# Seven products instead of eight in six more blocks of a hybrid encoder layer's matrix products, and two more first weight blocks on ScalarE's queue

## The chip, the cores and the metric

The kernel runs on one core of one Trainium2 chip. Its time is the device time of one execution in microseconds (us). A core has five engines that work side by side, each through its own queue, in order: TensorE (PE, with PEld for the weight load that runs ahead of a matmul), VectorE (DVE), ScalarE (ACT), GpSimd (POOL) and SyncE (SP, which here only issues transfers). Matmuls add into banks of PSUM; everything else is in SBUF tiles. A matmul of a 128x128 stationary tile with 128x512 moving columns is the unit of the matrix work below.

## The reference, cut to what matters

One layer over 256 positions of 2048 channels, all in float32:

```python
u = rmsnorm(h, norm_mix[l])
z = u @ w_in[l]                       # 2048 x 11264: pool, q, k, v, ret. gate, two branch gates
y_pool = pool_branch(p, w_pool_group[l], pool_scale[l]) @ w_pool_proj[l]
y_ret = retention_branch(q, k, v, g_ret, ret_gn_gain[l]) @ w_ret_proj[l]
merged = jax.nn.sigmoid(g_pool_br) * y_pool + jax.nn.sigmoid(g_ret_br) * y_ret
h = h + merged @ w_out[l]
h = h + conv_glu(rmsnorm(h, norm_ffn[l]), w_up[l], conv_w[l], conv_b[l], w_down[l])
out = rmsnorm(h, norm_final)
```

The retention branch normalizes each head's result (a group norm), multiplies it by a silu gate and goes through `w_ret_proj`. The feed-forward part has 5632 channels, `w_up` twice that. Nearly all arithmetic is in the products with `w_in`, `w_ret_proj`, `w_out`, `w_up` and `w_down`, and all their weights (285.8 MB read in all) are used once.

## The kernel before, in words

**Three matmuls for one product.** To keep float32 accuracy, each operand is split into a high part (`hi`, rounded) and the rest (`lo`). `mm3` makes a product from three matmuls: high by high (L104), high weights by low activations (L105), low weights by high activations (L106). Weights come from memory as raw blocks of 128x2048 (1 MB, pool `wraw`, three buffers) and are split on the way: ACT copies 1024 columns into a `hi` tile (L96), DVE subtracts for the `lo` tile (L97). The pools `hi` and `lo` have four buffers of 1024 columns each. A buffer comes free with the last matmul that reads it, and the next block's split waits for that.

**Groups.** One raw block is a *group*: 256 rows of the inner dimension by 1024 output columns, 2x2 quarters of weights against 2x2 quarters of activations (two halves of the positions, `tb`). A *pair* (`run_pair`, `down_pair`) is 1024 output columns with all its groups: eight for `w_in` (eleven pairs), `w_ret_proj` (two) and `w_out` (two), 22 for `w_down` (two pairs). A plain group is eight products, 24 matmuls. A group that is listed as a *Strassen group* takes seven products, 21 matmuls (`Pair.seven`, `Pair.strassen`): sums of weight quarters are made on DVE (L304 128x1024, L306 and L311 128x512) and split like the rest, with a tile `four` (128x512 high and low together) that takes a buffer of the `hi` pool, and a tile for the sums `t13` from the pool `units`. The products come in the order p1, p2, p6, p3, p7, p5, p4; p1 and p2 read the first `hi` tile, p6 and p3 the second, p7 and p5 the split `t13`, p4 the tile `four`. Four of them (p1, p5, p6, p7) add up over all Strassen groups of a pair in four PSUM banks of their own; after the last such group `fix_steps` or `h_steps` (L437, L351) add them to the results.

**Sums of activations.** The products p6, p3, p7 and p5 need sums of activation quarters. `sums_of` prepares them once for each group number of `w_in` (used by all its pairs), of `w_ret_proj` and of `w_out`: L360 forms hi+lo, `sums` (L344 to L347) adds on DVE, then ACT and DVE split. For `w_down` they are made while `w_up` runs.

**What sets the order.** Work beside the matrix products (the retention itself, rotations, norms, transposes, the sums) is in closures in a list, `side`; `run_pair` takes one after each group (`tick`), and `flush` the rest. The engines' instruction streams are fixed ahead of time by a scheduler that lists the work by readiness and by priority: weight loads and splits come 128 places early (`weights_first`), result steps 64 (`results_first`). So the order within an engine's queue differs from the order of the source, and at run time each engine takes its queue strictly in order.

**The pairs of `w_in`, counted from 0:** 0 and 3 are q and k (first and second half of the heads), 1 and 4 are v, 2 and 5 the retention gate, 6 the pool input, 7 and 8 the pool branch's gate, 9 and 10 the retention branch's gate. Pair 0 runs as the input arrives: `load_x` and `load_w` (L159 to L165) issue the first transfers in a fixed order, the ones that follow on SP.

**The end.** The two pairs of `w_down` follow `w_up`, whose 44 steps (L878 with 128x512, L886 with 128x256) make the activations in 22 groups; `plain_a` and `sums_a` say where each group's are stored.

Of the kernel before, what the change touches and what calls it, by code (L numbers as in the profile page):

```python
# [9 lines left out]
F32R = mybir.dt.float32r  # L10
# [6 lines left out]
P = 128  # L17
D = 2048
T = 256
# [14 lines left out]
STRASSEN = (2, 4, 6, 8, 11, 13, 16, 18)  # L34
STRASSEN_Z = (1, 3, 5)
STRASSEN_R = (1, 3, 5)
# [12 lines left out]
def tile_block(ctx: ExitStack, tc: tile.TileContext, ins, out):  # L49
# [119 lines left out]
    tc.keep_in_program_order(load_w(0, 2, 1))  # L169
    tc.keep_in_program_order(load_x(1, 1))  # L170
    tc.keep_in_program_order(load_w(0, 0, 1))
    tc.keep_in_program_order(load_w(0, 3, 1))
# [180 lines left out]
    def sums_of(pair_hl, groups):  # L353

        dst = [unit(F32R), unit(F32R)]

        def of(i, g):
            f = t2k()
            o = slice(g % 4 * NB, (g % 4 + 1) * NB)
            dve.tensor_tensor(f, *(plain(x[g // 4][:, o]) for x in pair_hl), ALU.add)  # L360
            a11, a21, a12, a22 = (f[:, j * P : (j + 1) * P] for j in range(4))
            sums(a11, a12, a21, a22, [x[:, i * NB : (i + 1) * NB] for x in dst])

        s4 = {
            g: [[z[:, i * NB + j * P : i * NB + (j + 1) * P] for z in dst] for j in range(4)]
            for i, g in enumerate(groups)
        }
        return s4, [lambda i=i, g=g: of(i, g) for i, g in enumerate(groups)]
# [228 lines left out]
    def group_norm(half, o_all, mv, sg):  # L597
# [35 lines left out]
        side.append(lambda: (scale(), apply(0)))  # L633
        side.append(lambda: apply(1))
        side.append(lambda: apply(2))
        side.append(lambda: (turn((0, 1)), apply(3)))
# [9 lines left out]
    for half in range(2):  # L646
        qk = [unit(F32R), unit(F32R)]
        qk_pair(qk, STRASSEN_Z[2:] if half else (), None if half else first)
        vh, vl = unit(F32R), unit(F32R)
        if half == 0:  # L650
            zs, fill = sums_of((uh, ul), STRASSEN_Z)
            side.extend(fill)
        split_pair(vh, vl, STRASSEN_Z[1:2] if half else ())
# [3 lines left out]
        gate_pair(sg, AF.Silu, STRASSEN_Z[1:], apart=True)  # L657
# [5 lines left out]
    split_pair(ph, pl, STRASSEN_Z[1:2])  # L663
# [66 lines left out]
    for dst in (sgp, sgp, sgr, sgr):  # L730
        dst.append(unit())
        gate_pair(dst[-1], AF.Sigmoid, STRASSEN_Z if len(sgp) > 1 else STRASSEN_Z[2:])
# [20 lines left out]
    side.extend(fill)  # L753
    for p in range(2):
# [21 lines left out]
        if p == 0:  # L776
            os, fill = sums_of((mg_h, mg_l), STRASSEN_O)
            side.extend(fill)
# [72 lines left out]

    ah = [unit(F32R) for _ in range(7)]
    al = [unit(F32R) for _ in range(7)]
    plain_groups = [g for g in range(NFF // 2) if g not in STRASSEN]
# [7 lines left out]
    def sums_a(g, c):  # L862

        n = STRASSEN.index(g)
        o = n % 2 * 7 * P
# [3 lines left out]
    for j in range(NFF):  # L869
# [51 lines left out]
        else:  # L921
            dve.tensor_tensor(cs[:, 2 * P :], c, u, ALU.mult)
            a21, a11, a12, a22 = (cs[:, i * P : (i + 1) * P] for i in range(4))
            split(*sums_a(grp, slice(0, 3 * P)), cs[:, P:])
# [241 lines left out]
```

## Time and profile before

| | |
|---|---|
| three timed runs, median (lowest to highest) | 1454.62 us (1453.79 to 1455.55) |
| the profiled execution's own time | 1455.32 us |
| its span in the trace | 1453.5 us, so 1.8 us lie outside it |
| PE busy | 1442.0 us, 99% |
| DVE busy | 1178.4 us, 81% |
| ACT busy | 794.3 us, 55% |
| mean granted TensorE clock | 0.998 |
| read from memory | 285.82 MB, 200 GB/s over the span |

The busy rows give the sum of an engine's instruction times, their share of the span and the number of instructions. A row of the groups gives line, engine, operation, out<-in, shapes, a count, then the busy time of the group, the mean of one in ns, and the idle time just before them with what ended most of it. A row of a timeline gives the start in us, the duration in us, engine, line, operation, out<-in, shapes and a count; in brackets at its end stands the idle time before it and what ended that. A matmul's duration is longer than the distance to the next, since they overlap.

### The profile page before, as it was taken

How to read it: one execution, taken by the hardware profiler on the slowest of the kernel's cores; microseconds unless marked ns; L12 is line 12 of the kernel's file. 1: busy time of each engine (PE TensorE's matmuls, PEld its weight loads, DVE VectorE, ACT ScalarE, POOL GpSimd, SP SyncE). 2: the span in 40 equal slices, each digit the busy share in tenths (PEclk: the TensorE clock that was granted, in tenths of full speed). 3: DMA queues.
4: the chain of work that ended last, by engine and by line, in shares of the span. 5: the costliest groups of instructions: out<-in, count | busy, mean ns of one | idle time of the engine just before them, and what ended most of it. 6: DMA issues, size and time to landing. Idle time of an engine off the chain costs nothing.

```text
span 1453.5 us, 18725 instructions
## 1 busy us (share of the span) xinstructions
PE 1442.0 (99%) x7163; PEld 1221.0 (84%) x7163; DVE 1178.4 (81%) x1638; ACT 794.3 (55%) x1023; POOL 0.2 (0%) x4
## 2 busy tenths in 40 slices
PE   9999999999999999999999999999999999999997
PEld 6888888888888888888888888888888888888886
DVE  6778797987988888988877787777777778888877
ACT  6555654565665555555555555554555555555553
POOL 0000000000000000000000000000000000000000
PEclk9999999999999999999999999999999999999999
DMA  9664455554555656555555445545554556665663
GB/s 352 214 218 174 154 197 193 192 205 179 181 201 196 229 177 217 213 204 203 213 210 204 184 176 200 204 175 179 207 194 174 187 205 239 209 216 186 220 217 117
DMA packets 43289, 291.22 MB, mean 200 GB/s; under 512 B 4928, under 2 KB 5568, under 8 KB 9152
## 3 DMA queue, kind: packets, MB, share of 16 engines
q1 hardware_dynamic: 42480, 288.73, 55.3%
q10 hardware_dynamic: 720, 1.31, 0.3%
q8 instruction: 56, 0.92, 0.2%
q14 instruction: 33, 0.27, 0.0%
HBM read 285.82 MB, written 4.19 MB: 200 GB/s over the span
## 4 chain that ended last, share of the span: by engine, by line
PE 97%; DVE 1%; DMA 1%; ACT 0%; SPq 0%; issue 0%; DVEq 0%; ACTq 0%
PE acc L878 22%; PE acc L106 15%; PE acc L104 15%; PE acc L105 15%; PE acc L886 12%; PE aux L104 6%; PE aux L106 6%; PE aux L105 6%; DMA raw<-in_w_in 1%; DVE lo L97 1%; PE aux L804 0%; PE aux L526 0%; PE aux L744 0%; PE aux L623 0%; DVE u L351 0%; PE aux L687 0%
## 5 line engine op out<-in xcount | busy, mean ns | idle before, releaser
L96 ACT ACTIVATE hi<-raw 128x1024 fp32r<-128x1024 f32 (+1 forms) x522 | 545.8, 1052 | 404.5 <-PE acc L105 183.0
L97 DVE TENSOR_TENSOR lo<-raw,hi 128x1024 fp32r<-128x1024 f32 (+1 forms) x522 | 618.1, 1214 | 155.8 <-ACT hi L96 98.4
L104 PE MATMUL acc<-hi,u 128*128 128x512 f32 x926 | 362.1, 391 | 1.5 <-ACT hi L96 1.5
L106 PE MATMUL acc<-lo,u 128*128 128x512 f32 x926 | 360.8, 390 | 0.0
L105 PE MATMUL acc<-hi,u 128*128 128x512 f32 x926 | 360.5, 389 | 0.0
L878 PE MATMUL acc<-u,hi 128*128 128x512 f32 x1408 | 328.4, 390 | 0.0
L878 PEld LDWEIGHTS acc<-u,hi 128*128 128x128 f32 x1408 | 261.3, 188 | 52.2
L104 PEld LDWEIGHTS acc<-hi,u 128*128 128x128 f32 x926 | 173.9, 188 | 37.6 <-ACT hi L96 2.4
L106 PEld LDWEIGHTS acc<-lo,u 128*128 128x128 f32 x926 | 173.8, 188 | 37.5 <-DVE lo L97 1.3
L105 PEld LDWEIGHTS acc<-hi,u 128*128 128x128 f32 x926 | 173.9, 188 | 35.2
L886 PEld LDWEIGHTS acc<-u,lo 128*128 128x128 f32 x1408 | 174.8, 192 | 3.4
L886 PE MATMUL acc<-u,lo 128*128 128x256 f32 x1408 | 176.0, 283 | 0.0
L104 PE MATMUL aux<-hi,u 128*128 128x512 f32 x270 | 105.3, 390 | 0.0
L105 PE MATMUL aux<-hi,u 128*128 128x512 f32 x270 | 105.1, 389 | 0.0
L106 PE MATMUL aux<-lo,u 128*128 128x512 f32 x270 | 105.1, 389 | 0.0
L900 ACT ACTIVATE t<-acc 128x256 f32<-128x256 f32 x88 | 33.9, 385 | 100.1 <-PE acc L886 100.1
L96 ACT ACTIVATE u<-u 128x1024 fp32r<-128x1024 f32 x45 | 47.5, 1057 | 26.7 <-DVE u L304 22.3
L106 PEld LDWEIGHTS aux<-lo,u 128*128 128x128 f32 x270 | 50.7, 188 | 10.6
L104 PEld LDWEIGHTS aux<-hi,u 128*128 128x128 f32 x270 | 50.7, 188 | 10.5 <-ACT hi L96 0.2
L105 PEld LDWEIGHTS aux<-hi,u 128*128 128x128 f32 x270 | 50.7, 188 | 10.4
L96 ACT ACTIVATE four<-raw 128x512 fp32r<-128x512 f32 x43 | 27.2, 632 | 55.4 <-PE acc L105 20.8
L97 DVE TENSOR_TENSOR u<-u,u 128x1024 fp32r<-128x1024 f32 x45 | 54.9, 1221 | 3.1 <-ACT u L96 3.1
(181 smaller groups left out, 1098.2 us busy)
## 6 DMA issues: line engine op xcount, KB each, us to landing
raw<-in_w_up SPq DMA_DIRECT2D x88, 1024.0 KB, 5.0
raw<-in_w_in SPq DMA_DIRECT2D x85, 1024.0 KB, 4.9
raw<-in_w_down SPq DMA_DIRECT2D x44, 1024.0 KB, 4.9
raw<-in_w_ret_proj SPq DMA_DIRECT2D x16, 1024.0 KB, 4.9
raw<-in_w_out SPq DMA_DIRECT2D x16, 1024.0 KB, 4.9
raw<-in_w_pool_proj SPq DMA_DIRECT2D x8, 1024.0 KB, 4.9
u<-in_x SPq DMA_DIRECT2D x4, 1024.0 KB, 7.6
raw<-in_w_in SPq DMA_DIRECT2D x4, 512.0 KB, 8.4
```

The lines of the kernel that those rows point to most:

```text
L96: act.activation(hi, src, AF.Copy)
L97: dve.tensor_tensor(lo, src, plain(hi), ALU.subtract)
L104: pe.matmul(o, ah, bh, start=start, stop=False)
L105: pe.matmul(o, al, bh, start=False, stop=False)
L106: pe.matmul(o, ah, bl, start=False, stop=stop)
L878: pe.matmul(o[half], w2[half][hf][0][:, i * P : (i + 1) * P], hview(kt), start=kt == 0, stop=False)
L886: pe.matmul(o[half][:, :T], wl, hview(kt)[:, :T], start=False, stop=kt == KT - 1)
L900: act.activation(small_part[:, half * T : (half + 1) * T], o[half][:, T:], AF.Copy)
```

## The change

It enlarges the lists of Strassen groups: in the second q and k pair (group 5 becomes 4 and 5), in the second retention gate (3 and 5 become 3, 4 and 5), in both `w_ret_proj` pairs (1, 3, 5 become 1, 2, 4, 5) and in both `w_down` pairs (eight groups become nine, now every second group from 2 to 18). That is six groups more. The sums of activations of group 1 of `w_in`, which only the pairs 8 to 10 read, leave the list that runs during pair 1 (the sums for group 4 take their place there) and are made at the end of pair 7 or later. The ninth sums of `w_down` are stored in tiles that are free by then (`front`, `trig`, `trig_r` and what the last `ah`/`al` tiles have left), which takes one split more. The side work of the group norm is regrouped into fewer steps. At the start two 128x512 quarters of the first weight block are issued by ACT's queue instead of SP's.

```diff
-STRASSEN = (2, 4, 6, 8, 11, 13, 16, 18)
-STRASSEN_Z = (1, 3, 5)
-STRASSEN_R = (1, 3, 5)
+STRASSEN = (2, 4, 6, 8, 10, 12, 14, 16, 18)
+STRASSEN_Z = (1, 3, 4, 5)
+STRASSEN_R = (1, 2, 4, 5)
 STRASSEN_O = (2, 3)
...
     tc.keep_in_program_order(load_w(0, 1, 1, act))
-    tc.keep_in_program_order(load_w(0, 2, 1))
+    tc.keep_in_program_order(load_w(0, 2, 1, act))
     tc.keep_in_program_order(load_x(1, 1))
     tc.keep_in_program_order(load_w(0, 0, 1))
-    tc.keep_in_program_order(load_w(0, 3, 1))
+    tc.keep_in_program_order(load_w(0, 3, 1, act))
...
-        return s4, [lambda i=i, g=g: of(i, g) for i, g in enumerate(groups)]
+        return s4, {g: lambda i=i, g=g: of(i, g) for i, g in enumerate(groups)}
...
-        side.append(lambda: (scale(), apply(0)))
-        side.append(lambda: apply(1))
-        side.append(lambda: apply(2))
-        side.append(lambda: (turn((0, 1)), apply(3)))
+        side.append(lambda: (scale(), apply(0), apply(1)))
+        side.append(lambda: (apply(2), apply(3)))
+        side.append(lambda: turn((0, 1)))
         side.append(lambda: None)
         side.append(lambda: turn((2, 3)))
...
-        qk_pair(qk, STRASSEN_Z[2:] if half else (), None if half else first)
+        qk_pair(qk, (4, 5) if half else (), None if half else first)
         vh, vl = unit(F32R), unit(F32R)
         if half == 0:
             zs, fill = sums_of((uh, ul), STRASSEN_Z)
-            side.extend(fill)
-        split_pair(vh, vl, STRASSEN_Z[1:2] if half else ())
+            side.extend(fill.pop(g) for g in (3, 5, 4))
+        split_pair(vh, vl, (3,) if half else ())
...
-        gate_pair(sg, AF.Silu, STRASSEN_Z[1:], apart=True)
+        gate_pair(sg, AF.Silu, (3, 4, 5) if half else (3, 5), apart=True)
...
-        gate_pair(dst[-1], AF.Sigmoid, STRASSEN_Z if len(sgp) > 1 else STRASSEN_Z[2:])
+        if len(sgp) == 1:
+            side.append(fill.pop(1))
+        gate_pair(dst[-1], AF.Sigmoid, (1, 3, 5) if len(sgp) > 1 else (5,))
         flush()
...
     ah = [unit(F32R) for _ in range(7)]
     al = [unit(F32R) for _ in range(7)]
+    a1 = [const.tile([P, n], F32R, tag=tag, name=f"a1_{tag}") for tag, n in (("front", KT + T), ("trig", T))]
+    last22 = const.tile([P, T], F32R, tag="trig_r", name="last22")
...
         n = STRASSEN.index(g)
+        if n == 8:
+            if c.start >= 3 * P:
+                o = (22 % 8) * T - 3 * P
+                return [x[6][:, o + c.start : o + c.stop] for x in (ah, al)]
+            if c.start == 2 * P:
+                return [last22[:, :P], last22[:, P:]]
+            return [x[:, c] for x in a1]
...
-            split(*sums_a(grp, slice(0, 3 * P)), cs[:, P:])
+            for c in (slice(0, 2 * P), slice(2 * P, 3 * P)) if grp == STRASSEN[-1] else (slice(0, 3 * P),):
+                split(*sums_a(grp, c), cs[:, P + c.start : P + c.stop])
```

**Where the order moves: pair 8, the second pool gate, on DVE.** Of the change, from the low part of group 3's first half: raw_646 is group 3's raw block, lo_649 and lo_651 its two low tiles, four_653 its `four`; t_617 and t_618 are the sums of activations of group 1; raw_654 is group 4, lo_656 its first low tile, raw_659 is group 5.

```order
L97 TENSOR_TENSOR lo_649_3461<-raw_646_3456,hi_648_3460 128x1024
L101 SCALAR_TENSOR_TENSOR u_539_2890<-aux_616_3296,vecs_237,u_538_2889 128x256
L311 TENSOR_TENSOR raw_646_3456<-raw_646_3456 128x512
L97 TENSOR_TENSOR lo_651_3466<-raw_646_3456,hi_650_3465 128x1024
L360 TENSOR_TENSOR t_617_3325<-u_5_104,u_7_106 128x512
L344 TENSOR_TENSOR t_618_3327<-t_617_3325 128x128
L97 TENSOR_TENSOR four_653_3473<-raw_646_3456,four_653_3473 128x512
L345 TENSOR_TENSOR t_618_3327<-t_618_3327,t_617_3325 128x128
L304 TENSOR_TENSOR u_660_3533<-raw_659_3531 128x1024
L346 TENSOR_TENSOR t_618_3327<-t_617_3325 128x128
L97 TENSOR_TENSOR lo_656_3500<-raw_654_3497,hi_655_3499 128x1024
```

Of before, the same place (raw_638 is group 3's block there, raw_646 group 4's, raw_651 group 5's):

```order
L97 TENSOR_TENSOR lo_641_3438<-raw_638_3433,hi_640_3437 128x1024
L101 SCALAR_TENSOR_TENSOR u_533_2876<-aux_610_3282,vecs_237,u_532_2875 128x256
L97 TENSOR_TENSOR lo_643_3443<-raw_638_3433,hi_642_3442 128x1024
L311 TENSOR_TENSOR raw_638_3433<-raw_638_3433 128x512
L97 TENSOR_TENSOR four_645_3450<-raw_638_3433,four_645_3450 128x512
L304 TENSOR_TENSOR u_652_3510<-raw_651_3508 128x1024
L306 TENSOR_TENSOR raw_651_3508<-raw_651_3508,u_652_3510 128x512
L97 TENSOR_TENSOR lo_648_3477<-raw_646_3474,hi_647_3476 128x1024
```

The sums of group 1 (L360, L344 and on) now stand behind group 3's low tiles; before, they stood in pair 1.

**On PE in the same pair,** the change reads: two products of group 3 (p1 and p2 with hi_648), its p4 (four_653), and the first halves of group 4 (hi_655) and, further on, its second (hi_657), ahead of group 1's p6, which reads group 1's second tile hi_637 and the sums u_70:

```order
L104 MATMUL acc_620_3339<-hi_648_3460,u_5_104 128x512
L105 MATMUL acc_620_3339<-hi_648_3460,u_7_106 128x512
L106 MATMUL acc_620_3339<-lo_649_3461,u_5_104 128x512
L104 MATMUL acc_622_3341<-four_653_3473,u_5_104 128x512
L105 MATMUL acc_622_3341<-four_653_3473,u_7_106 128x512
L106 MATMUL acc_622_3341<-four_653_3473,u_5_104 128x512
L104 MATMUL acc_620_3339<-hi_655_3499,u_6_105 128x512
...
L104 MATMUL acc_623_3342<-hi_657_3503,u_6_105 128x512
L105 MATMUL acc_623_3342<-hi_657_3503,u_8_107 128x512
L104 MATMUL aux_631_3379<-hi_637_3390,u_70_473 128x512
L104 MATMUL acc_621_3340<-hi_637_3390,u_70_473 128x512
```

Of before, p2 of group 1 (hi_627), then its p6 and p3 (hi_629 is its second tile) and, a few rows on, its `four`:

```order
L104 MATMUL acc_612_3316<-hi_627_3362,u_5_104 128x512
L105 MATMUL acc_612_3316<-hi_627_3362,u_7_106 128x512
L106 MATMUL acc_612_3316<-lo_628_3363,u_5_104 128x512
L104 MATMUL aux_623_3356<-hi_629_3367,u_70_473 128x512
L105 MATMUL aux_623_3356<-hi_629_3367,u_71_474 128x512
...
L104 MATMUL acc_614_3318<-four_632_3375,u_5_104 128x512
```

The products of group 1 that need sums have moved from their own group to the middle of group 4; hi_637 is read by nothing earlier.

**Pair 5, the second retention gate, on DVE.** Of the change, from group 3's `four` (four_426): raw_427 is group 4's block, a Strassen group now, raw_435 group 5's.

```order
L97 TENSOR_TENSOR four_426_2254<-raw_419_2237,four_426_2254 128x512
L97 TENSOR_TENSOR lo_430_2283<-raw_427_2278,hi_429_2282 128x1024
L97 TENSOR_TENSOR lo_432_2288<-raw_427_2278,hi_431_2287 128x1024
L311 TENSOR_TENSOR raw_427_2278<-raw_427_2278 128x512
L304 TENSOR_TENSOR u_436_2321<-raw_435_2319 128x1024
L97 TENSOR_TENSOR four_434_2295<-raw_427_2278,four_434_2295 128x512
L97 TENSOR_TENSOR lo_438_2324<-raw_435_2319,hi_437_2323 128x1024
L306 TENSOR_TENSOR raw_435_2319<-raw_435_2319,u_436_2321 128x512
L97 TENSOR_TENSOR u_441_2332<-u_436_2321,u_441_2332 128x1024
```

Of before (raw_424 is the plain group 4, raw_429 group 5):

```order
L97 TENSOR_TENSOR four_423_2247<-raw_416_2230,four_423_2247 128x512
L97 TENSOR_TENSOR lo_426_2274<-raw_424_2271,hi_425_2273 128x1024
L97 TENSOR_TENSOR lo_428_2278<-raw_424_2271,hi_427_2277 128x1024
L97 TENSOR_TENSOR lo_432_2310<-raw_429_2305,hi_431_2309 128x1024
L97 TENSOR_TENSOR lo_434_2315<-raw_429_2305,hi_433_2314 128x1024
L311 TENSOR_TENSOR raw_429_2305<-raw_429_2305 128x512
L571 TENSOR_TENSOR t_406_2203<-aux_405_2196,u_371_2042 128x384
```

Group 5's L304 and L306 stood ahead of this stretch before; now they stand in it, behind group 4's work.

**The second `w_ret_proj` pair, on DVE.** Of the change: raw_958 is group 1's block, raw_966 group 2's (a Strassen group now), raw_974 group 3's.

```order
L304 TENSOR_TENSOR u_967_5091<-raw_966_5089 128x1024
L97 TENSOR_TENSOR four_965_5065<-raw_958_5048,four_965_5065 128x512
L306 TENSOR_TENSOR raw_966_5089<-raw_966_5089,u_967_5091 128x512
L97 TENSOR_TENSOR u_972_5102<-u_967_5091,u_972_5102 128x1024
L97 TENSOR_TENSOR lo_969_5094<-raw_966_5089,hi_968_5093 128x1024
L344 TENSOR_TENSOR t_944_4971<-t_943_4969 128x128
L97 TENSOR_TENSOR lo_971_5099<-raw_966_5089,hi_970_5098 128x1024
L311 TENSOR_TENSOR raw_966_5089<-raw_966_5089 128x512
...
L304 TENSOR_TENSOR u_980_5166<-raw_979_5164 128x1024
L97 TENSOR_TENSOR four_973_5106<-raw_966_5089,four_973_5106 128x512
L97 TENSOR_TENSOR lo_976_5133<-raw_974_5130,hi_975_5132 128x1024
```

Of before (raw_953 is the plain group 2, raw_958 group 3):

```order
L304 TENSOR_TENSOR u_959_5086<-raw_958_5084 128x1024
L97 TENSOR_TENSOR four_952_5026<-raw_945_5009,four_952_5026 128x512
L306 TENSOR_TENSOR raw_958_5084<-raw_958_5084,u_959_5086 128x512
L97 TENSOR_TENSOR u_964_5097<-u_959_5086,u_964_5097 128x1024
L97 TENSOR_TENSOR lo_955_5053<-raw_953_5050,hi_954_5052 128x1024
...
L97 TENSOR_TENSOR lo_957_5057<-raw_953_5050,hi_956_5056 128x1024
```

The same sums of weights now belong to the group that PE takes next, a group earlier than before, and group 2's L311, group 4's L304 and group 2's `four` come ahead of group 3's low tile.

More of the change, by code (lines that the diff above doesn't have):

```diff
@@ L662, in tile_block @@
     ph, pl = unit(F32R), unit(F32R)
-    split_pair(ph, pl, STRASSEN_Z[1:2])
+    split_pair(ph, pl, (3,))
     flush()
@@ L752, in tile_block @@
     rs, fill = sums_of((ret_h, ret_l), STRASSEN_R)
-    side.extend(fill)
+    side.extend(fill.values())
     for p in range(2):
@@ L777, in tile_block @@
             os, fill = sums_of((mg_h, mg_l), STRASSEN_O)
-            side.extend(fill)
+            side.extend(fill.values())
     ht = [unit(F32R) for _ in range(4)]
```

## The prediction

> **What bounds the kernel now.** I read the page's busy rows first, then its chain of waits, then the waits of PE alone.
>
> ```profile
> PE 1442.0 (99%) x7163; PEld 1221.0 (84%) x7163; DVE 1178.4 (81%) x1638; ACT 794.3 (55%) x1023; POOL 0.2 (0%) x4
> ...
> PE 97%; DVE 1%; DMA 1%; ACT 0%; SPq 0%; issue 0%; DVEq 0%; ACTq 0%
> ...
> L96 ACT ACTIVATE hi<-raw 128x1024 fp32r<-128x1024 f32 (+1 forms) x522 | 545.8, 1052 | 404.5 <-PE acc L105 183.0
> L97 DVE TENSOR_TENSOR lo<-raw,hi 128x1024 fp32r<-128x1024 f32 (+1 forms) x522 | 618.1, 1214 | 155.8 <-ACT hi L96 98.4
> ...
> L105 PE MATMUL acc<-hi,u 128*128 128x512 f32 x926 | 360.5, 389 | 0.0
> ```
>
> ```profile
> 738.15 7.28 PE acc L878 x32
> ```
>
> ```profile
> PE acc L104 <- ACT hi L96: 1.5, 2, 0.9
> PE aux L181 <- DVE warm L176: 1.2, 1, 1.2
> PE aux L834 <- DVE dg L833: 0.2, 1, 0.2
> ```
>
> PE is the bound: busy 99%, 97% of the chain, and in all it waits for other engines 1.5 + 1.2 + 0.2 us. So a matmul taken away is worth its distance to the next, 7.28/32 = 0.2275 us (the 389 ns of the group row contain the overlap), as long as weights stay ready. And since nothing waits now, every new wait is added in full. DVE at 81% looks like room, but that is an average; whether it holds is a question to each stage. These are the stages that get more groups, by busy time in stretches (length, then PE, PEld, DVE, ACT, POOL, then clock, DMA share and GB/s): the second retention gate (pair 5), the second pool gate (pair 8), the second and the first `w_ret_proj` pair, the down pairs.
>
> ```profile
> 254.00:266.00 12.00, 12.00 (x61) 9.76 (x60) 12.00 (x16) 6.38 (x8) 0.00 (x0) 1.00 0.48 174
> 388.00:402.00 14.00, 14.00 (x64) 11.53 (x63) 12.24 (x14) 8.55 (x11) 0.00 (x0) 1.00 0.65 226
> 594.00:620.00 26.00, 26.00 (x116) 21.29 (x115) 25.59 (x32) 14.82 (x16) 0.00 (x0) 1.00 0.69 266
> 534.00:560.00 26.00, 26.00 (x117) 21.52 (x116) 20.31 (x20) 14.22 (x16) 0.00 (x0) 1.00 0.58 202
> 1330.00:1420.00 90.00, 90.00 (x399) 74.53 (x398) 76.66 (x80) 52.38 (x58) 0.00 (x0) 1.00 0.58 202
> ```
>
> DVE is full already in pair 5 (12.00 of 12.00) and in the second `w_ret_proj` pair (25.59 of 26.00). There a Strassen group is no longer free.
>
> **The price of a group on both sides.** PE saves three matmuls a group: 18 in six groups, 18 x 0.2275 = **-4.1 us**. On DVE a plain group is two low tiles; a Strassen group four operations of 1024 columns (L304, two low tiles, that of t13) and three of 512 (L306, L311, that of `four`). The distances in a full DVE queue:
>
> ```profile
> 258.91 4.63 DVE L97 TENSOR_TENSOR lo<-raw,hi 128x1024 fp32r<-128x1024 f32 x4
> 263.45 0.69 DVE L311 TENSOR_TENSOR raw<-raw 128x512 f32<-128x512 f32 x1
> 264.05 0.56 DVE L571 TENSOR_TENSOR t<-aux,u 128x384 f32<-128x384 f32 x1
> ```
>
> Four of 1024 take 4.63 - 0.09 to the next start, so 1.14 each; 512 columns take 264.05 - 263.45 = 0.60. So a plain group costs DVE 2.27 us under 24 matmuls of 5.46, a Strassen group 4 x 1.14 + 3 x 0.60 = 6.36 under 21 of 4.78: **1.6 us more than PE gives it**. Alone it lives on a lead; two or three in a row have to come from leads that the group before has eaten.
>
> **Hidden parts.** Down now alternates Strassen and plain up to group 18: DVE 6.36 + 2.27 = 8.63 under 45 matmuls of 10.24, so 0 (without that cover it would be 1.6 a group). The first `w_ret_proj` pair has DVE 20.31 of 26.00 and one group more (+4.1 - 0.7 of PE), which fits: 0; so do pair 4 and the up stage's one split more. Group-norm steps keep their instructions. Nobody waits for them within a pair.
>
> **The head**, from the timelines of the queues, ACT and PE:
>
> ```profile
> 0.72 0.41 ACTq L165 DMA_DIRECT2D raw<-in_w_in  x1
> 1.17 0.42 SPq L165 DMA_DIRECT2D raw<-in_w_in  x1
> 1.16 1.28 ACT L178 ACT_TABLE_LOAD   x1 [1.16 <-PEq L1155]
> 4.42 0.51 ACT L100 ACTIVATE u<-front 128x256 fp32r<-128x256 f32 x1 [1.76 <-DMA front<-in_xt]
> 11.12 0.39 PE L106 MATMUL acc<-lo,u 128*128 128x512 f32 x1
> 12.43 0.50 PE L104 MATMUL acc<-hi,u 128*128 128x512 f32 x1 [0.93 <-ACT hi L96]
> 12.77 0.40 PE L105 MATMUL acc<-hi,u 128*128 128x512 f32 x1
> ```
>
> Two issues leave SP, so all behind them go out up to 2 x 0.47 (slot: 0.42 and the gap to the next) = 0.94 earlier. Two issues more ahead of ACT's table load move its end from 2.44 to about 3.4, still before 4.42, where ACT waits for data: no loss. The one wait to gain from is 12.43 - (11.12 + 0.23) = 1.08, for the second weight block. But in that stretch the transfers already fill the engines:
>
> ```profile
> 6.00:12.00 6.00, 5.50 (x23) 4.05 (x22) 3.36 (x7) 2.79 (x6) 0.00 (x0) 1.00 1.00 333
> ```
>
> A DMA share of 1.00 says that bytes set the landing. Bounds: -1.2 (the whole wait and a little of the first) to +0.3 (ACT late after all). I take **-0.5**. The Trainium skill, "DMA: Bandwidth & Descriptors", section "Issuing engines are not separate DMA queues", says that issuing from several engines saves only the sequencer's time to start the transfer, as all share the same 16 engines; by it the term is near 0, and the trace's share of 1.00 agrees.
>
> **Pair 8.** The sums of group 1 (L360, L344 and on) stand on DVE behind group 3's low tiles, and PE takes group 1's p6, p3, p7, p5 only in the middle of group 4. Until then hi_637 and the second tiles of groups 2 and 3 hold three of four `hi` buffers. One buffer is left for first tile of 3, `four`, first of 4, second of 4, one after the other. Durations, from the timelines of ACT and DVE:
>
> ```profile
> 395.83 0.63 ACT L96 ACTIVATE four<-raw 128x512 fp32r<-128x512 f32 x1 [2.13 <-PE acc L105]
> 388.32 1.06 ACT L96 ACTIVATE hi<-raw 128x1024 fp32r<-128x1024 f32 x1 [0.18 <-PE acc L105]
> 597.22 1.22 DVE L304 TENSOR_TENSOR u<-raw 128x1024 f32<-128x1024 f32 x1
> 607.86 0.69 DVE L97 TENSOR_TENSOR four<-raw,four 128x512 fp32r<-128x512 f32 x1
> ```
>
> Clock from group 3's first matmul: the fifth matmul ends at 4 x 0.2275 + 0.39 = 1.30; then ACT 0.63, `four` high 1.96 (needed at 6 x 0.2275 = 1.37); DVE 0.69, its low 2.7; third matmul of p4 ends 2.7 + 0.5 = 3.2 (0.50 is a matmul after a wait, row of 12.43); buffer free, ACT 1.06, group 4's first tile 4.3 (needed 2.05); DVE 1.22, low 5.55; fifth matmul of group 4 there; the eleventh ends at about 7.5; ACT 1.06, second tile 8.55, PE at 8.6. Needed: 21 x 0.2275 = 4.78. So 3.8 late; the high part of the sums is behind it on ACT (0.2 more) and the spacing after a wait is 12.77 - 12.43 = 0.34 for 0.23: **+4.1**. Bounds: 3.4 (six steps each 0.1 shorter, no extra spacing) to 4.7 (0.1 longer).
>
> **Pair 5: groups 3, 4 and 5 in a row.** From the start 258.91 above, with the order of the change: two low tiles of group 4 until 261.2, L311 261.8, L304 of group 5 262.95, `four` of 4 263.55, low tile of 5 264.7, L306 265.3. Only after it may ACT make group 5's second high tile: 266.4. PE:
>
> ```profile
> 259.75 0.39 PE L104 MATMUL acc<-hi,u 128*128 128x512 f32 x1
> ```
>
> Group 4 starts there; 12 matmuls, three of `four` and six of group 5 later PE wants that tile: 259.75 + 21 x 0.2275 = 264.5. Late: 1.9, with respacing **+2.0**. Bounds: 0.2, if the lead is as where two Strassen groups stand side by side today (first `w_out` pair, second group's first matmul; the distance is 0.39 where 0.23 is normal, 0.16 lost):
>
> ```profile
> 653.14 0.41 PE L104 MATMUL aux<-hi,u 128*128 128x512 f32 x1
> 653.53 0.50 PE L104 MATMUL aux<-u,u 128*128 128x512 f32 x1
> ```
>
> to 2.6 (side work, the L571 of 0.56, slips in front).
>
> **Second `w_ret_proj` pair.** From 597.22 DVE runs through: L304, `four` of 1, L306, t13, two low tiles of group 2 with L344 (0.2) until 603.2, L311 603.8, L345 and L346 604.2, L304 of group 4 605.3, `four` of 2 605.95, first low tile of group 3 607.1. PE:
>
> ```profile
> 602.27 0.39 PE L104 MATMUL aux<-hi,u 128*128 128x512 f32 x1
> ```
>
> Group 2 starts there with nine matmuls, `four` at 604.3 (high ready after L311 and ACT 0.63: 604.5), then group 3's first tile at 604.8 by PE's pace; ACT makes it at 604.5 + 1.06 = 605.6, 0.7 late; its low tile is wanted five matmuls after that start, at 605.9, and ends at 607.1 + 0.09 = 607.2: 1.3 late in all. Later p7 needs the PSUM bank that ACT's copy of p1 (L437) has to free:
>
> ```profile
> 178.68 0.57 ACT L437 ACTIVATE t<-aux 128x512 f32<-128x512 f32 x1
> ```
>
> +0.6, and respacing 0.2: **+2.1**; bounds 0.2 (as in `w_out`) to 2.7 (that copy behind a high tile).
>
> **Second q and k, groups 4 and 5 in a row:** two, not three, with DVE short by 2 x 1.6 against leads of 1 to 3 us: **+0.3** (0 to 0.6).
>
> **Sum:** -4.1 - 0.5 + 4.1 + 2.0 + 2.1 + 0.3 = +3.9 on the profiled 1455.32 (span 1453.5 and 1.8 around it): 1459.2. The three runs' median is 0.7 below the profiled one: **1458.5**.
>
> **The rivals.** *Leads carry the rows of Strassen groups.* Pair 5, the second `w_ret_proj` and q and k lose 0.2 each or less, as `w_out` shows; pair 8 stays: -4.1 - 0.5 + 4.1 + 0.4 = -0.1, 1454.5 as a median. For it: no group waits today except that 0.16. Against it: DVE at 12.00 of 12.00 has no slack to build a lead. 0.32.
>
> *The other side: the `hi` buffer doesn't bind in pair 8.* If ACT and DVE are so far ahead that the freed buffer is refilled at once (the 2.13 and 0.18 us that ACT waits for PE in the rows of 395.83 and 388.32 show it ready early), and the leads carry the rest, -4.1 - 0.5 + 0.4 = -4.2: 1450.4. It decides from a chain under 1.4 us. Against it: the sum of the chain is ACT and DVE time behind PE, which being early can't shorten. 0.07.
>
> *The clock falls at the waits.* This kernel's mean granted clock is 0.998, so 0.002 x 1453.5 = 2.9 us are the price of what lowering it has; another such spell in pair 8's stops: 1458.5 + 2.9 = 1461.4. Against it: with a wait of 1.08 the row 6:12 has clock 1.00. 0.05. The Trainium skill, "TensorE: Matmul & The Clock Gate", section "HAM oscillation — how this bites in real kernels", has the clock lowered by gaps of more than about 3.4 us; no single stop that I expect is so long, so by it this rival falls.
>
> That the change doesn't do what it says is ruled out: the instruction order has 18 matmuls fewer.
>
> **How the numbers follow.** Forecast 0.56, rivals 0.32, 0.07, 0.05. A measurement can tell 0.2%, 2.9 us, from no change: slower is above 1457.5, faster below 1451.7. The forecast's own range is 1456.9 to 1461.2 (the terms' bounds don't all fall to one side), a tenth of it under 1457.5; with the clock's 0.05 slower has 0.56. Same: 0.32 and that tenth (0.05), less 0.01 for a better head: 0.36. Faster: 0.07 + 0.01 = 0.08. The range: 1453.8, under most of the first rival, to 1461.3; about 0.2 is left out.
>
> **What would show it.** Right: PE waits of 3 us or more in the second pool gate on ACT's high tiles of group 4 and DVE's low, around L360 and L344; some 2 us on ACT's second tile of group 5 in pair 5; 2 us in the second `w_ret_proj`; PE busy about 4 us less if busy time leaves waits out; the wait at 12 us shorter by about 0.5. Wrong: pair 8 without a wait, or a stage costed at nothing (down, first `w_ret_proj`) with one; any clock under 1.00 in those stretches.

## The result: slower, by twice what was forecast

The change takes 1462.56 us (four runs, 1461.04 to 1464.0) where the kernel before takes 1454.26 (1453.79 to 1455.55): ratio 1.0055, interval 1.0038 to 1.0073. Slower was forecast, but at 1458.5 with 1461.3 as the upper end. The profiled execution took 1464.0 (span 1462.2), 8.7 more than that of before. Its four times lie on two levels, 1461.1 and 1463.9; the granted clock is 0.999 in the lower two, 0.996 in the upper two.

The profile after, page first (busy rows, shares of the chain), then the waits of PE (total us, times, longest):

```profile
PE 1444.6 (99%) x7145; PEld 1219.3 (83%) x7145; DVE 1207.5 (83%) x1686; ACT 804.5 (55%) x1038; POOL 0.2 (0%) x4
...
PE 95%; DVE 3%; ACT 1%; issue 0%; DMA 0%; DVEq 0%; ACTq 0%
```

```profile
PE aux L104 <- ACT hi L96: 4.0, 4, 2.5
PE acc L104 <- ACT hi L96: 2.4, 3, 1.1
PE aux L181 <- DVE warm L176: 1.2, 1, 1.2
PE acc L104 <- ACT four L96: 0.5, 1, 0.5
PE acc L104 <- ACT t L437: 0.5, 1, 0.5
PE aux L104 <- ACT four L96: 0.2, 1, 0.2
```

18 matmuls are gone, and yet PE's busy time has risen by 2.6 us: some matmuls run slowly. And PE, which before waited only at the start and for 0.2 us near the end, now waits 4.0 + 2.4 + 0.5 + 0.5 + 0.2 = 7.6 us in all behind ACT, 0.35 of it still at the start. Where these waits stand, in PE's timeline (start, duration, in brackets the idle time and what ended it), pair 5, pair 6, pair 8 and the second `w_ret_proj` pair:

```profile
262.42 0.50 PE L104 MATMUL aux<-hi,u 128*128 128x512 f32 x1 [0.21 <-ACT hi L96]
265.45 0.50 PE L104 MATMUL aux<-hi,u 128*128 128x512 f32 x1 [1.04 <-ACT hi L96]
...
303.86 0.39 PE L106 MATMUL acc<-lo,u 128*128 128x512 f32 x1
306.73 0.50 PE L104 MATMUL aux<-hi,u 128*128 128x512 f32 x1 [2.48 <-ACT hi L96]
...
307.65 0.63 PE L105 MATMUL acc<-hi,u 128*128 128x512 f32 x1
308.08 0.63 PE L104 MATMUL aux<-u,u 128*128 128x512 f32 x1
...
400.83 0.50 PE L104 MATMUL acc<-four,u 128*128 128x512 f32 x1 [0.54 <-ACT four L96]
403.20 0.79 PE L104 MATMUL acc<-hi,u 128*128 128x512 f32 x1 [1.15 <-ACT hi L96]
408.60 0.51 PE L104 MATMUL acc<-hi,u 128*128 128x512 f32 x1 [0.91 <-ACT hi L96]
...
613.58 0.50 PE L104 MATMUL aux<-four,u 128*128 128x512 f32 x1 [0.19 <-ACT four L96]
614.53 0.50 PE L104 MATMUL aux<-hi,u 128*128 128x512 f32 x1 [0.22 <-ACT hi L96]
616.11 0.50 PE L106 MATMUL aux<-lo,u 128*128 128x512 f32 x1 [0.15 <-DVE lo L97]
627.55 0.50 PE L104 MATMUL acc<-u,u 128*128 128x512 f32 x1 [0.46 <-ACT t L437]
```

The distance between two starts beyond 0.2275 is what a place costs. The first distance after a wait is longer too (0.34 where 0.23 is normal); that is called the start-up here. For 306.73 that is 306.73 - 303.86 - 0.23 = 2.64. Added up with the start-ups: pair 5 2.0 (0.4 of it stood there before), pair 6 2.75, pair 8 3.7, the second `w_ret_proj` pair 2.05. Besides, behind the wait of pair 6 matmuls stand 308.08 - 307.65 = 0.43 apart instead of 0.23, and the same behind 403.20. In windows (length, then PE, PEld, DVE, ACT, POOL, then the granted clock):

```profile
300.00:306.00 6.00, 4.25 (x23) 3.27 (x21) 3.02 (x6) 3.24 (x6) 0.00 (x0) 1.00 0.00 0
306.00:312.00 6.00, 5.27 (x18) 4.14 (x19) 4.79 (x7) 4.10 (x6) 0.00 (x0) 0.72 0.00 0
400.00:406.00 6.00, 4.31 (x12) 2.70 (x11) 5.70 (x9) 2.63 (x3) 0.00 (x0) 0.74 0.63 223
```

A clock of 0.72 and 0.74 over six microseconds: the slow distances fill some three of them (307.3 to 310.6 in the first). The distances beyond 0.23 add up to 1.6 us behind the wait of pair 6 and 1.4 in pair 8, 3.0 in all, about the 2.8 between the two levels of times.

Where the time went, by the starts of the same instructions in both traces (in the last row the end of the last matmul), in us:

| point in the program | before | after | difference | step since the row above, and what it is |
|---|---|---|---|---|
| first rotation transposes, pair 0 (L526) | 72.67 | 71.88 | -0.8 | the head |
| stretch before pair 5, a matmul with a start-up | 241.80 | 240.61 | -1.2 | -0.4: q and k +0.3, and -0.7 of matmuls |
| pair 7, the same kind of place | 342.00 | 346.33 | +4.3 | +5.5: pair 5 (+1.0) and pair 6 (+4.4) |
| transposes behind the first `w_ret_proj` pair | 576.01 | 584.92 | +8.9 | +4.6: pair 8 (+5.1) and -0.7 of matmuls |
| transposes behind the second | 641.16 | 651.49 | +10.3 | +1.4: stalls 2.05, -0.7 of matmuls |
| last matmul's end | 1445.03 | 1453.72 | +8.7 | -1.6: down, -1.4 of matmuls |

Every saved matmul arrived; the rows leave 0.1 to 0.2 us each without a place. Of the stalls all but one were forecast to within 0.5 us. The one that was not is in pair 6, which has no added Strassen group.

### The profile page after: what moved, and what is told of

It is laid out like the page before. It is cut to its first block, busy times and chain, and to the rows that moved or that the text cites. A ratio compares the mean times of both kernels' runs of the same rounds, so it can differ in the third digit from the quotient of the medians.

```text
span 1462.2 us, 18753 instructions
## 1 busy us (share of the span) xinstructions
PE 1444.6 (99%) x7145; PEld 1219.3 (83%) x7145; DVE 1207.5 (83%) x1686; ACT 804.5 (55%) x1038; POOL 0.2 (0%) x4
## 4 chain that ended last, share of the span: by engine, by line
PE 95%; DVE 3%; ACT 1%; issue 0%; DMA 0%; DVEq 0%; ACTq 0%
PE acc L889 22%; PE acc L104 15%; PE acc L105 15%; PE acc L106 15%; PE acc L897 11%; PE aux L104 6%; PE aux L106 6%; PE aux L105 5%; DVE lo L97 1%; DVE u L304 0%; DVE u L97 0%; ACT hi L96 0%; DMA raw<-in_w_in 0%; PE aux L745 0%; PE aux L805 0%
## 5 line engine op out<-in xcount | busy, mean ns | idle before, releaser
L104 PE MATMUL acc<-hi,u 128*128 128x512 f32 x912 | 358.0, 393 | 2.4 <-ACT hi L96 2.4
L105 PE MATMUL acc<-hi,u 128*128 128x512 f32 x912 | 356.4, 391 | 0.0
L106 PE MATMUL acc<-lo,u 128*128 128x512 f32 x912 | 355.1, 390 | 0.0
L104 PEld LDWEIGHTS acc<-hi,u 128*128 128x128 f32 x912 | 171.9, 189 | 38.9 <-ACT hi L96 4.1
L105 PEld LDWEIGHTS acc<-hi,u 128*128 128x128 f32 x912 | 172.0, 189 | 34.9
L104 PE MATMUL aux<-hi,u 128*128 128x512 f32 x256 | 100.5, 393 | 4.0 <-ACT hi L96 4.0
L106 PE MATMUL aux<-lo,u 128*128 128x512 f32 x256 | 100.0, 391 | 0.2 <-DVE lo L97 0.2
L105 PE MATMUL aux<-hi,u 128*128 128x512 f32 x256 | 99.7, 390 | 0.0
L96 ACT ACTIVATE u<-u 128x1024 fp32r<-128x1024 f32 x51 | 53.8, 1054 | 23.5 <-DVE u L304 18.8
L304 DVE TENSOR_TENSOR u<-raw 128x1024 f32<-128x1024 f32 x49 | 59.6, 1217 | 5.9 <-DMA raw<-in_w_down 5.7
L97 DVE TENSOR_TENSOR u<-u,u 128x1024 fp32r<-128x1024 f32 x51 | 62.1, 1218 | 1.9 <-ACT u L96 1.9
L96 ACT ACTIVATE four<-raw 128x512 fp32r<-128x512 f32 x49 | 31.0, 632 | 57.3 <-DVE raw L311 25.9
L104 PEld LDWEIGHTS aux<-hi,u 128*128 128x128 f32 x256 | 48.1, 188 | 15.7 <-ACT hi L96 5.8
```

The costliest lines, as they stand in the source:

```text
L96: act.activation(hi, src, AF.Copy)
L97: dve.tensor_tensor(lo, src, plain(hi), ALU.subtract)
L104: pe.matmul(o, ah, bh, start=start, stop=False)
L105: pe.matmul(o, al, bh, start=False, stop=False)
L106: pe.matmul(o, ah, bl, start=False, stop=stop)
L304: dve.tensor_tensor(t13, raw[:, 2 * NB :], raw[:, NB : 3 * NB], ALU.subtract)
```

## The experiments

The comparisons stand against the kernel before on the same chip, 1454.4 to 1454.7 in the three sets. Differences to the change itself reach across sets; the kernel before stood at 1454.26 in that one.

**What blocks pair 6.** ACT and DVE of the change at that place:

```profile
295.27 2.07 ACT L614 ACTIVATE u<-u,mr,y 128x256 f32<-128x256 f32 x4
302.47 1.50 ACT L100 ACTIVATE u<-aux,vecs 128x256 fp32r<-128x256 f32 x3 [5.14 <-PE aux L623]
303.87 0.59 ACT L437 ACTIVATE t<-aux 128x512 f32<-128x512 f32 x1
304.63 1.06 ACT L96 ACTIVATE u<-u 128x1024 fp32r<-128x1024 f32 x1 [0.17 <-DVE u L304]
305.62 1.06 ACT L96 ACTIVATE hi<-raw 128x1024 fp32r<-128x1024 f32 x1
```

```profile
296.54 1.42 DVE L615 TENSOR_TENSOR u<-u,u 128x256 f32<-128x256 f32 x4
302.98 0.48 DVE L101 SCALAR_TENSOR_TENSOR u<-aux,vecs,u 128x256 fp32r<-128x256 f32 x1 [5.02 <-ACT u L100]
303.38 1.21 DVE L304 TENSOR_TENSOR u<-raw 128x1024 f32<-128x1024 f32 x1
```

ACT idles 5.14 us and DVE 5.02 us, and behind them in their queues stand the sums of weights (L304) and the high tiles of group 3. What they wait for is a transpose on PE (L623, 301.84), which stands at the end of group 2 in PE's queue: the regrouped group norm puts `turn((0, 1))` and its splits (L100, L101) ahead of the Strassen group, where before they came behind it. So the lead that ACT and DVE had is gone, and PE, at group 3's p6, waits for a tile that could have been made five microseconds earlier. Of before, ACT, then PE: group 3's `four` is ready before PE starts that group at 301.95, and the transposes come ten microseconds later:

```profile
300.15 0.62 ACT L96 ACTIVATE four<-raw 128x512 fp32r<-128x512 f32 x1
...
301.95 0.39 PE L104 MATMUL aux<-hi,u 128*128 128x512 f32 x1
...
312.15 1.03 PE L623 MATMUL aux<-ident,u 128*128 128x128 f32 x8
```

*The group norm's steps put back as they were, in the change:*

```diff
-        side.append(lambda: (scale(), apply(0), apply(1)))
-        side.append(lambda: (apply(2), apply(3)))
-        side.append(lambda: turn((0, 1)))
+        side.append(lambda: (scale(), apply(0)))
+        side.append(lambda: apply(1))
+        side.append(lambda: apply(2))
+        side.append(lambda: (turn((0, 1)), apply(3)))
```

> The change with the group norm's side work in its old steps. Theory (transposes ahead of a Strassen group): in the change the first transposes of the group norm (L623) stand right ahead of group 3 of pair 6; ACT and DVE, strictly in order, wait there for PE (5.14 and 5.02 us idle) and group 3's L304 and high tiles come 2.6 us late. With the old steps they stand behind that group in pair 6, and its stall of 2.64 goes; but in pair 3 they now stand right ahead of group 4, a Strassen group since the change, and a stall of about 2 to 2.6 us must appear there. The time stays within 1.5 us of the change. Rival (debt of DVE): the stall of pair 6 is what three Strassen groups in a row in pair 5 left over; then it stays at about 2.6 in pair 6 and nothing appears in pair 3. Clock theory: the granted clock falls behind a stall of over 2 us, so a stretch of matmuls 0.43 us apart follows the stall in pair 3.

1464.57 us (1463.77 to 1466.59), 2.0 more than the change (its median lies between two levels) and not within 1.5 as expected. But the stall did what the theory said: none in pair 6, and in pair 3, ahead of group 4, which is a Strassen group since the change:

```profile
169.04 1.03 PE L623 MATMUL aux<-ident,u 128*128 128x128 f32 x8
...
171.06 0.39 PE L106 MATMUL acc<-lo,u 128*128 128x512 f32 x1
174.00 0.61 PE L104 MATMUL aux<-hi,u 128*128 128x512 f32 x1 [2.54 <-ACT hi L96]
174.41 0.63 PE L105 MATMUL aux<-hi,u 128*128 128x512 f32 x1
```

The stall moved with the transposes: 174.00 - 171.06 - 0.23 = 2.71 where it was 2.64. The debt of DVE from pair 5 has no part in it. The low clock (0.43 between matmuls) came with it; pair 8's waits are there as in the change, but without a low clock (1.00 from 402 to 408 us). Part of the 2.0 shows in this one trace, the longest of the five: PE waits 0.75 and 0.22 us near the end of the second down pair, for the last weight block, for whose transfer ACT waits 1.66 us. The rest is open.

*The group norm's new steps alone, in the kernel before* (the same diff the other way round):

> The kernel before with only the group norm's new steps. Theory (transposes ahead of a Strassen group): the stall of pair 6 appears here too, without any added Strassen group: 2.3 to 2.8 us on ACT's high tile, and by the clock theory up to 1.6 more in some executions: 1456.5 to 1458.5. Rival (debt of DVE): nothing, within 0.5 us of the kernel before.

1458.71 us (1458.13 to 1459.25), ratio 1.0028 with an interval of 1.0017 to 1.0039, upper end of the theory's range and a little over. PE's waits there, without any added Strassen group:

```profile
PE aux L104 <- ACT hi L96: 2.5, 1, 2.5
PE aux L181 <- DVE warm L176: 1.2, 1, 1.2
PE acc L104 <- ACT hi L96: 0.9, 1, 0.9
```

So a few lines of the diff that look like tidying cost 4.3 us by themselves. Of these the trace shows 2.75, the wait of 2.48 with its start-up; the profiled execution had no lowered clock (1.00 from 306 to 312 us), and with 1458.13 it is the shortest of the seven. That the other six had a stretch of low clock is not shown: they are 0.4 to 1.1 us longer, less than the 1.6 of such a stretch.

The same trace says more exactly what must not be moved. In pair 3 the transposes of the second two heads (`turn((2, 3))`) stand right ahead of Strassen group 5 on PE, and nothing waits. ACT, then PE:

```profile
171.78 0.63 ACT L96 ACTIVATE four<-raw 128x512 fp32r<-128x512 f32 x1 [1.66 <-PE acc L105]
...
175.46 0.82 ACT L100 ACTIVATE u<-aux,vecs 128x256 fp32r<-128x256 f32 x2
...
174.48 1.03 PE L623 MATMUL aux<-ident,u 128*128 128x128 f32 x8
175.27 0.48 PE L104 MATMUL aux<-hi,u 128*128 128x512 f32 x1
```

Here the splits of the weights stood ahead of L100 in ACT's queue. What costs is not a transpose ahead of the group on PE, but the splits that wait for it ahead of the group's weights on ACT and DVE.

*New steps for the first half of the heads, old ones for the second, in the change:*

```diff
-        side.append(lambda: (scale(), apply(0), apply(1)))
-        side.append(lambda: (apply(2), apply(3)))
-        side.append(lambda: turn((0, 1)))
+        if half:
+            side.append(lambda: (scale(), apply(0)))
+            side.append(lambda: apply(1))
+            side.append(lambda: apply(2))
+            side.append(lambda: (turn((0, 1)), apply(3)))
+        else:
+            side.append(lambda: (scale(), apply(0), apply(1)))
+            side.append(lambda: (apply(2), apply(3)))
+            side.append(lambda: turn((0, 1)))
```

> The change with the group norm's new steps for the first half of the heads and the old ones for the second. Theory (transposes ahead of a Strassen group): no stall over 0.5 us in pair 3 nor in pair 6; 2.7 us less than the change by the stall, and up to 1.6 more by the stretch of low clock behind it: 2.7 to 4.3 us less. Rival (debt of DVE): pair 6 keeps its 2.6 us, time as of the change.

1458.98 us (1458.78 to 1460.66): 3.6 less than the change, inside the 2.7 to 4.3; no wait in pair 3 and none in pair 6. Its five times lie on two levels as well, three at 1458.8 to 1459.0 and two at 1460.5 to 1460.7; the profiled one is on the upper, and has a granted clock of 0.74 behind pair 8's waits.

**Pair 8.** *The sums of group 1 back in pair 1, in the change:*

```diff
-            side.extend(fill.pop(g) for g in (3, 5, 4))
+            side.extend(fill.pop(g) for g in (1, 3, 5, 4))
...
-        if len(sgp) == 1:
-            side.append(fill.pop(1))
```

> The change with the sums of group 1 made in pair 1, as before. Theory: the waits in pair 8 (0.70, 1.41 and 1.08 us and their start-up, 3.7 in all) go, and with them the stretch of low clock there (1.4): 3.7 to 5.1 us less than the change, unless the fourth sums in pair 1 cost something there (0 to 0.5). Rival: pair 8's waits come from the buffers that the Strassen groups share and stay, at least by half.

1458.39 us (1456.74 to 1458.84): 4.2 less than the change, as expected; pair 8 has no wait at all. The fourth sums cost nothing in pair 1. Its eleven times lie on two levels again, three at 1456.7 to 1457.1 and eight at 1458.4 to 1458.8, 1.6 apart. Pair 6's stall is the only one over 1.3 us left in this kernel; the profiled execution is one of the three, and its clock after that stall is 1.00.

**Both taken away.** *Group norm by halves, and the sums in pair 1:*

> The change with both causes taken away: the group norm's new steps for the first half of the heads alone, and the sums of group 1 in pair 1. Theory: the stalls of pair 6 (2.64 and 0.11 of start-up) and of pair 8 (3.7) are apart and add up, and with no stall over 1.5 us left the stretches of low clock go too: the undisturbed times of the change, 1461.1, less 6.45 is 1454.6, and the two levels of times, 1.6 us apart, become one. Rival (the stalls hide others behind them): over 1456.

1454.97 us (1454.62 to 1455.6), ratio 1.0003 (0.9995 to 1.0012): 7.6 less than the change, and the two causes alone gave 3.6 and 4.2. They add up, and nothing was hidden behind them. Eleven times within 1.0 us: one level. The longest waits that are left behind the start:

```profile
PE aux L104 <- ACT hi L96: 1.5, 3, 1.0
PE aux L106 <- DVE u L97: 0.6, 1, 0.6
PE acc L104 <- ACT t L437: 0.5, 1, 0.5
```

The first and the last are those of the rows of Strassen groups. The second stands at the last weight block of `w_down` (1435.01): ACT waits 0.96 us for that block's transfer. This wait comes and goes: it is in six of the thirteen traces, with 0.28 to 0.75 us, and not in that of the change.

**The rows.** *As that, with groups 3 and 5 in the second retention gate:*

```diff
-        gate_pair(sg, AF.Silu, (3, 4, 5) if half else (3, 5), apart=True)
+        gate_pair(sg, AF.Silu, (3, 5), apart=True)
```

> As the run with both causes taken away, and the second retention gate with groups 3 and 5 instead of 3, 4 and 5: three matmuls more (+0.68), its stalls of 0.38 and 1.21 with start-ups gone but for the 0.4 that stood there before (-1.65): 1.0 us less than that run, 1453.6. Rival: the debt of DVE only moves behind the pair, no difference or +0.7.

1453.64 us (1452.76 to 1455.43), 1.3 less; expected 1.0. In the traces the way from the first rotation transposes to those behind the first `w_ret_proj` pair is 1.4 shorter (502.18 instead of 503.54). The third group in a row costs more than its three matmuls bring.

*And `w_ret_proj` with 1, 3 and 5 again* (`STRASSEN_R = (1, 3, 5)`):

> As the run before it in this list, and the w_ret_proj pairs with groups 1, 3 and 5 again: six matmuls more (+1.37), the stalls in the second pair gone (0.35, 0.38, 0.32, 0.61 and their start-ups, -2.05): 0.7 less than that, about 1452.9. What is left of the change then are the q and k pair, the two down pairs (-2.05 in all) and the head. Rival: the first w_ret_proj pair loses as much as the second gains, 1454.3.

1453.74 us (1452.76 to 1454.64): no difference by the medians, where 0.7 was expected. In the profiled executions the last matmul starts at 1442.22 instead of 1443.08, 0.9 earlier (0.1 of it from the start), and the four waits of the second pair are gone. With times that spread over 1.9 and 2.7 us, 0.7 is not to be told; the traces show it, the times don't.

*Another choice for `w_ret_proj`: 1, 3, 4 and 5 in the first pair, 1, 3 and 5 in the second* (with the three edits before it: group norm by halves, sums in pair 1, pair 5 with 3 and 5):

```diff
-STRASSEN_R = (1, 2, 4, 5)
+STRASSEN_R = (1, 3, 4, 5)
...
-            lambda g: ins["w_ret_proj"][p * 8 + g], 8, (ret_h, ret_l), merge, STRASSEN_R, rs, fix_steps(fixed),
+            lambda g: ins["w_ret_proj"][p * 8 + g], 8, (ret_h, ret_l), merge, (1, 3, 5) if p else STRASSEN_R, rs, fix_steps(fixed),
```

> The change without its stalls (group norm's new steps for the first half alone, sums of group 1 in pair 1, second retention gate with groups 3 and 5), w_ret_proj with groups 1, 3, 4 and 5 in the first pair and 1, 3 and 5 in the second. Theory: as the run without the rows (1453.7) less three matmuls, 0.68: 1453.0, since DVE has room in the first w_ret_proj pair. Rival: three in a row stall there as in the second retention gate, 1.2 us or more: 1454.3.

1452.74 us (1451.28 to 1454.56) against 1454.67: ratio **0.9983, interval 0.9975 to 0.9992**. This is the version that beats both kernels, by 1.9 us the one before: four of the six added groups, the head, and none of the stalls. Its waits:

```profile
PE aux L181 <- DVE warm L176: 1.2, 1, 1.2
PE acc L104 <- ACT hi L96: 0.4, 1, 0.4
PE aux L839 <- DVE dg L838: 0.2, 1, 0.2
```

In the first `w_ret_proj` pair three in a row do not stall as they do in pair 5. Before the change DVE was busy 20.31 of 26.00 us there, and 12.00 of 12.00 in pair 5; that this room is the reason fits the forecast and was not tested apart.

**One group more, by the same rule.** *Group 1 of pair 7 as well:*

```diff
-        gate_pair(dst[-1], AF.Sigmoid, (1, 3, 5) if len(sgp) > 1 else (5,))
+        gate_pair(dst[-1], AF.Sigmoid, (1, 3, 5) if len(sgp) > 1 else (1, 5))
```

> As that, and group 1 a Strassen group in the first pool gate too (pair 7: 1 and 5 instead of 5), which the early sums allow. Theory: three matmuls less again, 1452.3, if the pool branch's side work on DVE in that pair leaves room. Rival: group 1 stands behind the side work there and PE waits 1 us or more: no gain.

1459.19 us (1458.97 to 1462.87), ratio 1.0039: 6.5 us more for three matmuls less. ACT, then PE, in its timelines:

```profile
333.73 2.01 ACT L96 ACTIVATE u<-u 128x1024 fp32r<-128x1024 f32 x2 [3.49 <-DMA u<-in_w_pool_group]
...
340.12 0.50 PE L104 MATMUL aux<-hi,u 128*128 128x512 f32 x1 [4.57 <-ACT hi L96]
```

It is pair 6's mechanism, with a transfer in place of the transposes. ACT's queue stands at the split of the pool branch's weights, which wait 3.49 us for their transfer, and group 1's high tiles stand behind. The place costs 4.73 us, and another 1.9 behind it, with a granted clock of 0.72 from 340 to 346 us. With a plain group 1 there (the version before this one) nothing waits, because ACT's queue has another order: high tiles at 331.37 and 334.10 stand ahead of that split, and when its turn comes the transfer has landed:

```profile
335.07 1.99 ACT L96 ACTIVATE u<-u 128x1024 fp32r<-128x1024 f32 x2
```

**The head.** *The kernel before with the two issues on ACT's queue alone:*

> The kernel before with the two first weight quarters issued by ACT's queue, nothing else. Theory (issue slots): the wait of 1.08 us at 12 us goes, the first matmul comes up to 0.5 later: 0.8 us less than before, 1453.6. Rival (bytes set the landing): within 0.2 of before.

1453.83 us (1453.59 to 1455.0) against 1454.38: 0.55 less, ratio 0.9998 with 0.9989 to 1.0006, so between the two expectations and not to be told from none by the runs. The trace is clearer: the wait of 1.08 us at 12 us is gone, the first matmul behind the warm-up starts at 5.97 instead of 5.50, and the first rotation transposes come at 71.71 instead of 72.67 (0.8 earlier in the change). Of the eleven traces with the two issues on ACT's queue nine have them at 71.4 to 72.0 and two, which begin with slow matmuls, at 73.6; the two traces without stand at 72.67. So a gain of about 1.0 is lost again in some executions, which would fit the smaller gain of the medians.

**The down pairs with the head.** *The kernel before with the nine groups of `w_down` and the two issues.* The change's own storage for the ninth group's sums is left out here: they lie over a plain group's activations, so the values differ and the work is the same.

> The kernel before with the two parts of the change that the theory holds for free: nine Strassen groups in each w_down pair, and the two first quarters on ACT's queue. Theory: six matmuls less (-1.37) and the head (-0.6 as measured alone): 2.0 less than before, 1452.4, with no new wait of PE in the down pairs. Rival: DVE's added 4.1 us a pair shows as waits in the down pairs, within 0.5 of the head alone, 1453.8.

1453.71 us (1452.56 to 1455.03) against 1454.67: 1.0 less (ratio 0.9994, 0.9985 to 1.0003) where 2.0 was expected; that is the rival's figure, and by the times alone the rival stands. The profiled execution, the longest of the eleven, has slow matmuls at the start (about 0.43 us apart from 6.7 to 10.2 us), which cost it 1.7 us. From the transposes behind the second `w_ret_proj` pair to the end of the last matmul its trace takes 802.69 us, where the kernel with the head alone takes 803.52. That is the -1.37 of six matmuls and one wait of 0.32 us (a distance 0.48 too long) at the last weight block, for whose transfer ACT waits 0.70 us. In the trace of the whole change that wait isn't there, and the part has its full -1.4 (last row of the table above). So the six matmuls arrive, and whether DVE's added work makes that last wait more frequent is open.

## Why the prediction was right and wrong, step by step

- **"18 x 0.2275 = -4.1"**: right. The table fits -0.7 for each group's three matmuls, -1.4 in down.
- **Pair 8, +4.1**: right in place and mechanism, 3.7 measured. Of the chain through one `hi` buffer all three waits are there, in the order forecast: on `four` (0.70 with its spacing), on group 4's first tile (1.41), on its second (1.08). With the sums made early they are gone. The rival that the buffer doesn't bind has fallen.
- **Pair 5, +2.0, and the second `w_ret_proj` pair, +2.1**: right in place, and in size to 0.4 (2.0, of which 0.4 was there before, so 1.6; and 2.05), by the waits that were named: ACT's second tile of group 5, `four`, the high and the low tile of group 3, and the PSUM bank that L437 frees. The rival that leads carry the rows has fallen there. It holds in the first `w_ret_proj` pair, as costed.
- **Second q and k, +0.3**: 0.3 by the table.
- **The head, -0.5**: 0.55 alone, 0.8 in the change's trace. The size is right, a reason for it isn't: the DMA share of 1.00 was read as a limit by bytes, but with the two issues on ACT's queue the same six microseconds move 402 GB/s at a share of 1.04 instead of 333 at 1.00.
- **"Group-norm steps keep their instructions. Nobody waits for them within a pair."** This is the step that failed. The instructions are the same, but one step, `turn((0, 1))`, changed sides of a Strassen group: its transposes on PE and the splits that wait for them. Nobody waits for their results; what waits is everything queued behind them. It costs 2.75 us in pair 6, put at 0 in the sum, and 4.3 by the medians in the kernel before alone. In ACT's queue L100 stands ahead of group 3's high tiles (302.47, then 304.63 and 305.62); the work was costed by its amount and its reader, not by what it stops.
- **The clock, given 0.05 and 2.9 us**: it came, in two of four runs, in the size given (2.8 between the levels, 3.0 by the distances). That the size fits is luck. The 2.9 was read from the mean granted clock of 0.998, but in the trace of before the clock is 1.00 up to 1446 us, and what lowers the mean is the end, where no matmul starts any more: 0.67 over its 8.5 us, so 0.33 x 8.5 = 2.8 us, which cost nothing. The 3.0 are two stretches of 1.6 and 1.4, one behind pair 6's stop, which the prediction did not have, and one behind pair 8's. The prediction let it fall because no single stop that was expected was near 3.4 us, by the Trainium skill, "TensorE: Matmul & The Clock Gate", section "HAM oscillation — how this bites in real kernels". Here a stop of 2.48 was enough in one trace of three (the change, not the early sums nor the group norm alone), one of 2.54 in another, and the cluster of 0.54 and 1.15 within 3 us in pair 8 in two of three (the change and the group norm by halves, not the old steps). The page and the measurement differ, and the measurement decides. With single waits of 1.04 and below alone, the eleven times of the version without both causes stayed on one level.

The row of that idle end, of before (length, then PE, PEld, DVE, ACT, POOL, then clock, DMA share and GB/s):

```profile
1445.00:1453.50 8.50, 0.03 (x1) 0.00 (x0) 3.50 (x13) 2.03 (x6) 0.00 (x0) 0.67 0.36 127
```

Adding up: against the forecast's +3.9 the head came out 0.3 lower, pair 8 and pair 5 0.4 each, and a wait of 0.24 near the end is gone, so the costed terms make +2.6. The step costed at nothing adds 2.75, which makes 5.3; the clock adds 3.0 in the executions where it is lowered: 8.3 of the 8.7 us between the two profiled executions. The rest is not placed, and the lower level of the change's times, 1461.1, is 6.9 above the median of before where 5.3 would do: 1.6 us there are open, for no trace of that level was kept. With the group norm costed at 2.75 the forecast would have been 1461.2, and with the clock 1464.

## What to carry to other kernels

A move of side work is costed by what stands behind it: on each engine that runs in order, find the first instruction of the moved step that waits for another engine or a transfer, and ask whose inputs are queued behind it. Work that needs a lead (here a Strassen group, which takes 1.6 us more of DVE than PE gives it) must not come right behind such an instruction in the queues of the engines that prepare it; on PE the order alone did no harm. Where a kernel's bound engine never waits, price a stop of some microseconds with its lowered clock too, here up to 1.6 us on top of 2.6, in some executions.

## What the runs showed of the hardware

The clock of TensorE falls after stops that are shorter than expected, and not each time. Behind the stop of 2.48 us in the change the first two distances were 0.34 and 0.23 as after any wait, then eight were 0.35 to 0.43, from 307.3 to 310.6; the clock was back at full after about 3.3 us of work. Behind the 2.54 in the run with the old steps the first distance is 0.41 already. With a stop of 2.48 again in the kernel with the early sums, three of eleven executions are 1.6 us shorter than the rest. That the two levels of times are these stretches is shown for the profiled executions alone (the change and the group norm by halves on the upper level with the stretch, the early sums on the lower without), since only they have a trace. The mean granted clock of a run can't stand in for it: the idle end alone takes 0.001 to 0.002 off it.

At the start of the program, matmuls at 0.43 apart appear in some executions and not in others, whether or not the kernel has stalls later: for none of the first matmuls in the trace of before, for about eight in that of the down pairs with the head (1.7 us). The granted clock in the rows is 1.00 in those windows, so there it doesn't show them. It may be much of the 1.0 to 3.3 us over which the times of the versions without the two causes spread, but only single executions have a trace. The Trainium skill, "TensorE: Matmul & The Clock Gate", section "What's actually happening", says that the number of slow first matmuls varies from run to run, and the traces agree (none and about eight; the first distance was 0.33 in one and 0.59 in another).
